# Hybrid decoder trunk: six gate buffers in place of four in the branch merge

## The chip, the cores and the metric

The kernel runs on one core of one Trainium2 chip. The metric is device microseconds (us) of one execution, lower is better. Three runs of the kernel before took 1336.45, 1338.84 and 1338.37 us, so the median is 1338.37 us. A profile was taken of one further execution.

The core has five engines, each with an instruction queue of its own that is worked off strictly in order: TensorE (PE; its weight loads are shown as PEld), VectorE (DVE), ScalarE (ACT), GpSimd (POOL) and SyncE (SP), which here only issues transfers. An instruction that waits holds up all that stand behind it on its engine.

## What is computed

One decoder layer on a 1024 x 1024 input in float32: a norm, one wide projection, two attention branches, a merge of the two by sigmoid gates, an output projection with a residual, and a gated feed-forward part. The change lies in the merge:

```python
y_da = diff_attention(da_q, da_k, da_v, lam, lam_init, subln_w[l])
y_sw = sliding_window_attention(sw_q, sw_k, sw_v, sinks[l])
merged = jax.nn.sigmoid(g_da) * (y_da @ w_br_da[l]) + jax.nn.sigmoid(g_sw) * (y_sw @ w_br_sw[l])
x = x + merged @ w_mix_out[l]
xn = rmsnorm(x, norm_ffn_w[l])
```

`g_da` and `g_sw` are columns of the projection. They were written to HBM before their norm factor was applied (tensor `gd`, 16 rows of 128 x 1024), so the merge loads them, multiplies them by `rstd` and takes the sigmoid.

## The kernel before

Everything is kept transposed: channels on the 128 partitions, the 1024 tokens along the free dimension. A product in full float32 precision is made of three matmuls on high and low parts (`h` and `l` tiles; the high part is a cast on ScalarE, the low part a subtraction on VectorE). 128 output channels are a block, so the merge has 8 blocks, numbered m = 0 to 7 here.

The merge is in `rest`. For each block, `first(m)` takes the next weight (`next_w`, which also has the weight after it loaded and split, lines 177 and 179), allocates two gate tiles of 512 KB with the tag `gr`, loads them on SP (line 796), scales them on GpSimd (line 797), takes the sigmoid on ScalarE (line 804), has TensorE make the 24 matmuls of the first branch (PSUM tile `sc`) and multiplies the first gate by it on VectorE (line 808). `second(m)` makes the 24 matmuls of the second branch in two halves (PSUM tiles `g`, two buffers, lines 212 to 214), multiplies each half of the second gate by it on VectorE (line 816), adds the two gates (line 821; GpSimd for blocks 0 to 5, VectorE for 6 and 7), and splits the sum into the high part `mh` on ScalarE (line 822) and the low part `ml` on VectorE (line 823). `first(0)` and `first(1)` are written ahead of `second(0)`; from block 2 on, `first(m)` and `second(m)` follow each other. TensorE's second-branch product of a block needs the `g` buffer that line 816 of the block before it frees.

The pool of the gate tiles has 4 buffers, two blocks' worth. A buffer is free again when its last reader is done: for a block's second gate that is the add of line 821, for its first gate the subtraction of line 823. The first gate of block m + 2 goes into the buffer of block m's second gate, and the second gate into that of the first.

The order on each engine is not the order of the code: a scheduler that works from estimated times places the instructions of each engine, and the order is then fixed.

After the merge comes `mix`: 8 blocks of 48 matmuls each on `mh` and `ml` (block numbers 0 to 7 again, called mix blocks here). For each, `x2` (a tile of the input, pool `xtp`) is loaded on SP (line 860), the product is added to it on VectorE (line 865), and it is squared, scaled and split for the feed-forward part. `xtp` lies in memory where the merge's pools lay; in the kernel before, the first two `x2` tiles lie just behind the four gate buffers and overlap none of them.

Of the kernel before, what the change touches and what calls it, by code (L numbers as in the profile page):

```python
# [17 lines left out]
P = 128  # L18
D = 1024
T = 1024  # L20
# [24 lines left out]
class Trunk:  # L45
# [723 lines left out]
    def rest(self, gctx):  # L769
        nc, tc = self.nc, self.tc  # L770
        with ExitStack() as ctx:
            e = ctx.enter_context
            mctx = ExitStack()
            mh, ml = [], []
            with gctx, ExitStack() as bctx:
                yrp = bctx.enter_context(tc.tile_pool(name="yrp", bufs=4, reuse_waits="tile"))
                yp = bctx.enter_context(tc.tile_pool(name="yp", bufs=1, reuse_waits="tile"))
                bp = bctx.enter_context(tc.tile_pool(name="bp", bufs=2, reuse_waits="tile"))
                parts = []
                for c in range(8):  # L780
                    with tc.high_priority(200):
                        r = self.tl(yrp, [P, T], "yr")
                        nc.sync.dma_start(r, self.yd[c])
                    parts.append(self.split(*(yp.tile([P, T], F32R, name=f"y{p}{c}") for p in "hl"), r))
                    if self.back[7][0]:
                        self.back_half(*self.back[7][0].pop(0))
                yact = [lambda kc, hf, o=o: [t[:, hf * H2:(hf + 1) * H2] for t in parts[o + kc]] for o in (0, 4)]
                self.xctx.close()
                mp = mctx.enter_context(tc.tile_pool(name="mp", bufs=1, side="right", reuse_waits="tile"))

                def first(m):
                    w = self.next_w()
                    gs = []
                    for br in range(2):
                        g = self.tl(bp, [P, T], "gr", bufs=4)
                        nc.sync.dma_start(g, self.gd[8 * br + m])
                        i = nc.gpsimd.tensor_tensor(g, g, self.rstd, ALU.mult)  # L797
                        if m == 0:

                            tc.add_manual_dep(i.ins, self.last.ins.name, mybir.DependencyInfo(mybir.DependencyClass.Sync, mybir.DependencyReason.DATA),  # L800
                                              reason="softmax first")

                        with tc.issue_after(self.hi.ins) if br else nullcontext():
                            nc.scalar.activation(g, g, AF.Sigmoid)
                        gs.append(g)
                    ps = self.tl(self.psS, [P, T], "sc")
                    self.mm3_both(ps, w, yact[0], range(4), late=() if m else range(4))
                    nc.vector.tensor_tensor(gs[0], gs[0], ps, ALU.mult)
                    return w, gs

                def second(m, w, gs):
                    for hf in range(2):
                        ps = self.tl(self.psG, [P, H2], "g")
                        self.mm3(ps, w, yact[1], hf, range(4), o=4)
                        g = gs[1][:, hf * H2:(hf + 1) * H2]
                        nc.vector.tensor_tensor(g, g, ps, ALU.mult)
                    a = mp.tile([P, T], F32R, name=f"mh{m}")
                    b = mp.tile([P, T], F32R, name=f"ml{m}")
                    with tc.high_priority(30) if m == KC - 1 else nullcontext():
                        for c in [slice(hf * H2, (hf + 1) * H2) for hf in range(2)] if m == KC - 1 else [slice(0, T)]:  # L820
                            (nc.vector if m >= KC - 2 else nc.gpsimd).tensor_tensor(gs[0][:, c], gs[0][:, c], gs[1][:, c], ALU.add)
                            nc.scalar.copy(a[:, c], gs[0][:, c])
                            nc.vector.tensor_tensor(b[:, c], gs[0][:, c], a[:, c].bitcast(F32), ALU.subtract)
                    mh.append(a)
                    ml.append(b)

                both = [first(m) for m in range(2)]
                for m in range(KC):
                    second(m, *(both[m] if m < 2 else first(m)))

            pair = self.mix(mh, ml, mctx)
            self.hidden(pair)
            self.down()
# [626 lines left out]
```

## Time and profile before

| what | value |
|---|---|
| runs | 1336.45, 1338.84, 1338.37 us, median 1338.37 us |
| profiled execution | 1338.85 us, span of its trace 1337.1 us |
| granted TensorE clock | 0.998 |
| busy share of the span | PE 99%, PEld 82%, DVE 79%, ACT 47%, POOL 37% |
| merge, first product to the start of mix | about 506 to 595 us of the span |
| HBM traffic | 130.66 MB read, 50.86 MB written |

In rows of a timeline the columns are the start in us from the start of the span, the length in us, the engine, the line, the operation, output and inputs with their shapes, and the number of instructions that one row merges; in brackets stands how long the engine sat idle before, and what ended that. In the chain of waits the columns are the start, the length and what the chain ran through. A row of waits has the instruction that waited, what it waited for, the total in us, the number of times and the longest one.

### The profile page before, as it was taken

Reading aid. Unit: us, or ns where it says so; the run is one execution under the profiler, and the core shown is the slowest. Engines: PE = TensorE matmul, PEld = TensorE weight load, DVE = VectorE, ACT = ScalarE, POOL = GpSimd, SP = SyncE. Lnnn points to the kernel's source line nnn. Section 1 sums busy time; section 2 is a strip of 40 time slices with the busy share of each in tenths; the row PEclk is TensorE's granted clock in tenths of the full one; section 3 lists DMA queues with packets and bytes.
Section 4 is the critical chain, followed back from the end, with each engine's and each line's share of the span. In section 5 each row is a group of like instructions: output and inputs, shape, how many; then the busy total and the mean of one; then the engine's idle time right before and its main releaser. Section 6 shows DMA issues by size and latency. Waiting matters only on the chain.

```text
span 1337.1 us, 17312 instructions
## 1 busy us (share of the span) xinstructions
PE 1319.5 (99%) x6264; PEld 1096.2 (82%) x6264; DVE 1062.9 (79%) x1601; ACT 623.2 (47%) x1023; POOL 500.9 (37%) x369
## 2 busy tenths in 40 slices
PE   8999999999999999999999999999999999999997
PEld 6888888888888778878888888888888888888887
DVE  8847775289888876456678899999999997878975
ACT  9432232176667765334445443344444444323554
POOL 0336543000002115651436556555565520214532
PEclk9999999999999999999999999999999999999999
DMA  6433443876553335334432222222222229672353
GB/s 259 146 106 145 155 158 142 244 185 177 155 130 121 106 113 210 142 111 144 140 111 82 92 87 87 79 79 95 79 95 71 80 83 327 212 281 73 95 173 126
DMA packets 63622, 183.70 MB, mean 137 GB/s; under 512 B 6960, under 2 KB 15280, under 8 KB 63536
## 3 DMA queue, kind: packets, MB, share of 16 engines
q1 hardware_dynamic: 51504, 164.13, 37.5%
q10 hardware_dynamic: 11456, 17.41, 3.6%
q0 software_dynamic: 576, 1.05, 0.4%
q8 instruction: 49, 0.80, 0.3%
q14 instruction: 37, 0.30, 0.1%
HBM read 130.66 MB, written 50.86 MB: 136 GB/s over the span
## 4 chain that ended last, share of the span: by engine, by line
PE 87%; POOL 4%; DMA 3%; DVE 3%; ACT 1%; issue 1%; POOLq 0%; SPq 0%; ACTq 0%; DVEq 0%
PE t L924 13%; PE t L925 13%; PE t L923 13%; PE t L917 3%; PE sc L639 3%; PE g L212 3%; PE g L213 3%; PE g L214 3%; PE y L1167 2%; PE d L1167 2%; DMA gr<-gd 2%; PE sc L214 2%; PE sc L213 2%; PE sc L212 2%; PE d L924 2%; PE d L923 2%
## 5 line engine op out<-in xcount | busy, mean ns | idle before, releaser
L1097 ACT ACTIVATE c<-us,vecs 128x512 f32<-128x512 f32 x80 | 61.3, 781 | 132.3 <-POOL us L1091 128.3
L1099 DVE SCALAR_TENSOR_TENSOR c<-us,vecs,c 128x512 f32<-128x512 f32 x160 | 110.4, 747 | 8.6 <-ACT c L1097 8.5
L1091 POOL TENSOR_TENSOR us<-us,rstd 128x1024 f32<-128x1024 f32 x38 | 99.6, 2640 | 4.5 <-DVE us L472 2.4
L129 DVE TENSOR_TENSOR sl<-sf,sh 128x1024 fp32r<-128x1024 f32 x62 | 86.6, 1399 | 11.5 <-ACT sh L128 11.5
L128 ACT CAST sh<-sf 128x1024 fp32r<-128x1024 f32 x62 | 63.4, 1047 | 60.3 <-PE t L924 44.0
L179 DVE TENSOR_TENSOR wl<-raw,wh 128x1024 fp32r<-128x1024 f32 (+2 forms) x46 | 56.2, 1221 | 30.7 <-ACT wh L177 19.1
L129 DVE TENSOR_TENSOR wl<-raw,wh 128x1024 fp32r<-128x1024 f32 (+1 forms) x35 | 76.6, 2189 | 3.7 <-ACT wh L128 3.6
L104 POOL TENSOR_TENSOR sf<-rv 128x512 f32<-128x512 f32 x30 | 41.3, 1375 | 101.9 <-DVE sl L129 57.8
L177 ACT CAST wh<-raw 128x1024 fp32r<-128x1024 f32 (+2 forms) x46 | 46.0, 1001 | 59.6 <-PE sc L213 30.5
L212 PE MATMUL g<-xh,wh 128*128 128x512 f32 x176 | 70.7, 401 | 0.1
L214 PE MATMUL g<-xh,wl 128*128 128x512 f32 x176 | 70.4, 400 | 0.0
L213 PE MATMUL g<-xl,wh 128*128 128x512 f32 x176 | 70.3, 400 | 0.0
L109 POOL TENSOR_TENSOR sf<-raw,rv 128x512 f32<-128x512 f32 x30 | 40.7, 1357 | 65.4 <-DVE sl L129 65.4
L622 POOL MEMSET aT<- 128x128 f32 x32 | 6.1, 204 | 151.6 <-PE t L668 97.9
L643 DVE CUSTOM_DVE_ANT_0 L<-sc,bias 128x128 f32<-128x128 f32 (+7 forms) x64 | 47.7, 751 | 17.0 <-PE sc L639 13.8
L644 ACT ACTIVATE L<-L,sm 128x128 f32<-128x128 f32 (+7 forms) x64 | 49.6, 778 | 20.0 <-DVE sm L643 17.3
L797 POOL TENSOR_TENSOR gr<-gr,rstd 128x1024 f32<-128x1024 f32 x16 | 41.0, 2570 | 42.0 <-DMA gr<-gd 41.8
L129 DVE TENSOR_TENSOR wl<-rv,wh 128x512 fp32r<-128x512 f32 x30 | 49.8, 1659 | 3.5 <-ACT wh L128 3.5
L1101 ACT ACTIVATE c<-c 128x512 f32<-128x512 f32 x40 | 24.0, 599 | 60.7 <-DVE c L1099 60.7
L639 PE MATMUL sc<-u,u 128*128 128x512 f32 (+2 forms) x192 | 49.6, 358 | 0.0
L214 PE MATMUL sc<-mh,wl 128*128 128x512 f32 x126 | 49.2, 390 | 0.4 <-DVE wl L179 0.4
L212 PE MATMUL sc<-mh,wh 128*128 128x512 f32 x126 | 49.1, 389 | 0.0
(530 smaller groups left out, 4397.6 us busy)
## 6 DMA issues: line engine op xcount, KB each, us to landing
u<-qd SPq DMA_DIRECT2D x72, 256.0 KB, 6.3
raw<-in_w_in SPq DMA_DIRECT2D x25, 512.0 KB, 4.1
raw<-in_w_up SPq DMA_DIRECT2D x23, 512.0 KB, 3.5
hr<-hd SPq DMA_DIRECT2D x46, 256.0 KB, 5.3
hd<-c SPq DMA_DIRECT2D x22, 512.0 KB, 2.6
rv<-in_w_up SPq DMA_DIRECT2D x21, 512.0 KB, 3.5
raw<-in_w_down SPq DMA_DIRECT2D x19, 512.0 KB, 4.3
gr<-gd SPq DMA_DIRECT2D x16, 512.0 KB, 3.7
```

The lines of the kernel that those rows point to most:

```text
L128: i = nc.scalar.copy(hi, src)
L129: j = nc.vector.tensor_tensor(lo, src, hi.bitcast(F32), ALU.subtract)
L212: nc.tensor.matmul(ps, wh[:, kc + o, :], ah, start=first and n == 0, stop=False)
L213: nc.tensor.matmul(ps, wh[:, kc + o, :], al, start=False, stop=False)
L214: nc.tensor.matmul(ps, wl[:, kc + o, :], ah, start=False, stop=last and n == len(kcs) - 1)
L639: nc.tensor.matmul(sc[:, lo + n0:lo + n1], qs, k[c][part][:, n0:n1], start=part == 0, stop=part == 1)
L923: nc.tensor.matmul(ps, ah[:, k, :], bh, start=first and n == 0, stop=False, skip_group_check=skip)
L924: nc.tensor.matmul(ps, ah[:, k, :], bl, start=False, stop=False, skip_group_check=skip)
L925: i = nc.tensor.matmul(ps, al[:, k, :], bh, start=False, stop=last and n == len(ks) - 1, skip_group_check=skip)
L1091: (nc.vector if j == 0 else nc.gpsimd).tensor_tensor(u[:, 2:], u[:, 2:], self.rstd, ALU.mult)
L1097: nc.scalar.activation(c, u[:, o + 2:o + 2 + H2], AF.Identity, bias=self.vecs[:, C_CB + m:C_CB + m + 1], scale=col(m, 2))
L1099: nc.vector.scalar_tensor_tensor(c, u[:, o + k:o + k + H2], col(m, k), c, ALU.mult, ALU.add)
```

## The change

The gate tiles get 6 buffers in place of 4, 8 KB more in each partition.

```diff
                     gs = []
                     for br in range(2):
-                        g = self.tl(bp, [P, T], "gr", bufs=4)
+                        g = self.tl(bp, [P, T], "gr", bufs=6)
                         nc.sync.dma_start(g, self.gd[8 * br + m])
                         i = nc.gpsimd.tensor_tensor(g, g, self.rstd, ALU.mult)
                         if m == 0:
```

No instruction is added or removed. The first gate of block m + 3 now goes into the buffer of block m's second gate, and the second into that of the first. The two new buffers lie where the first two `x2` tiles of `mix` lie: the first `x2` tile takes the place of the first gate of block 7, the second that of the second gate of block 6, so they can be loaded only when these are done with.

The orders of TensorE and VectorE are the same as before. GpSimd, ScalarE and SP are placed differently. In the rows below the two gates of a block have these numbers: block 0 5078 and 5082, block 1 5118 and 5122, block 2 5224 and 5228, block 3 5297 and 5301, block 4 5370 and 5374, block 5 5443 and 5447, block 6 5516 and 5520, block 7 5589 and 5593.

GpSimd at the beginning of the merge, from the scaling of block 1's gates on, before (L797 scales a gate, L821 adds a block's two gates):

```order
L797 TENSOR_TENSOR gr_5118<-gr_5118,rstd 128x1024
L797 TENSOR_TENSOR gr_5122<-gr_5122,rstd 128x1024
L821 TENSOR_TENSOR gr_5078<-gr_5078,gr_5082 128x1024
L797 TENSOR_TENSOR gr_5224<-gr_5224,rstd 128x1024
L821 TENSOR_TENSOR gr_5118<-gr_5118,gr_5122 128x1024
L797 TENSOR_TENSOR gr_5228<-gr_5228,rstd 128x1024
L797 TENSOR_TENSOR gr_5297<-gr_5297,rstd 128x1024
L797 TENSOR_TENSOR gr_5301<-gr_5301,rstd 128x1024
L821 TENSOR_TENSOR gr_5224<-gr_5224,gr_5228 128x1024
L797 TENSOR_TENSOR gr_5370<-gr_5370,rstd 128x1024
L797 TENSOR_TENSOR gr_5374<-gr_5374,rstd 128x1024
L821 TENSOR_TENSOR gr_5297<-gr_5297,gr_5301 128x1024
```

and the same stretch of the changed kernel:

```order
L797 TENSOR_TENSOR gr_5118<-gr_5118,rstd 128x1024
L797 TENSOR_TENSOR gr_5122<-gr_5122,rstd 128x1024
L797 TENSOR_TENSOR gr_5224<-gr_5224,rstd 128x1024
L797 TENSOR_TENSOR gr_5228<-gr_5228,rstd 128x1024
L821 TENSOR_TENSOR gr_5078<-gr_5078,gr_5082 128x1024
L797 TENSOR_TENSOR gr_5297<-gr_5297,rstd 128x1024
L821 TENSOR_TENSOR gr_5118<-gr_5118,gr_5122 128x1024
L797 TENSOR_TENSOR gr_5301<-gr_5301,rstd 128x1024
L797 TENSOR_TENSOR gr_5370<-gr_5370,rstd 128x1024
L797 TENSOR_TENSOR gr_5374<-gr_5374,rstd 128x1024
L821 TENSOR_TENSOR gr_5224<-gr_5224,gr_5228 128x1024
L797 TENSOR_TENSOR gr_5443<-gr_5443,rstd 128x1024
```

The two scalings of block 2 moved ahead of the add of block 0, and from there on each add stands behind the scalings of the block two after its own; before, it stood behind those of the block one after its own.

ScalarE at the end of the merge, a piece of the difference (L804 is a sigmoid, L177 the cast of a weight: 5510 is the branch weight of block 7, 5583 the first weight of `mix`; L822 makes `mh` of block 5):

```order
+L804 ACTIVATE gr_5589<-gr_5589 128x1024
 L177 CAST wh_5512<-raw_5510 128x1024
 L804 ACTIVATE gr_5520<-gr_5520 128x1024
 L822 CAST mh_5505<-gr_5443 128x1024
-L804 ACTIVATE gr_5589<-gr_5589 128x1024
 L177 CAST wh_5585<-raw_5583 128x1024
 L804 ACTIVATE gr_5593<-gr_5593 128x1024
```

The sigmoid of block 7's first gate moved from just ahead of the cast of the first `mix` weight to just ahead of the cast of the last branch weight.

SP, a piece of the difference around the loads of the first two `x2` tiles (x_992 and x_998):

```order
+L796 DMA gr_5593<-gd 128x1024
+L167 DMA raw_5773<-in_w_mix 128x1024
+L167 DMA raw_5852<-in_w_mix 128x1024
+L167 DMA raw_5919<-in_w_mix 128x1024
 L860 DMA x_992_5710<-in_xT 128x1024
 L860 DMA x_998_5771<-in_xT 128x1024
-L796 DMA gr_5224<-gd 128x1024
-L167 DMA raw_5364<-in_w_br 128x1024
-L796 DMA gr_5228<-gd 128x1024
```

Before, the two `x2` loads stood ahead of the gates of block 2, at the merge's start; now they stand behind the last gate and behind the weights of mix blocks 2 to 4, at the merge's end.

## The prediction

> **What bounds the kernel now.** I read the page first, then TensorE's own idle gaps in the merge, then who waits for whom there, then the chain of waits through it. The page's first part says who sets the end:
>
> ```profile
> PE 1319.5 (99%) x6264; PEld 1096.2 (82%) x6264; DVE 1062.9 (79%) x1601; ACT 623.2 (47%) x1023; POOL 500.9 (37%) x369
> ```
>
> TensorE is busy for 1319.5 of 1337.1 us. A change in the merge can win only what TensorE loses there, and it costs what it makes TensorE lose more. TensorE's timeline between 505 and 700 us has four rows with idle time before them:
>
> ```profile
> 522.89 0.50 PE L212 MATMUL g<-yh,wh 128*128 128x512 f32 x1 [0.44 <-DVE gr L816]
> 577.94 0.50 PE L212 MATMUL g<-yh,wh 128*128 128x512 f32 x1 [0.35 <-DVE gr L816]
> 589.64 0.50 PE L212 MATMUL g<-yh,wh 128*128 128x512 f32 x1 [0.52 <-DVE gr L816]
> 596.24 0.50 PE L214 MATMUL sc<-mh,wl 128*128 128x512 f32 x1 [0.41 <-DVE wl L179]
> ```
>
> That is 1.72 us of idle time; a matmul after a gap is also shown longer than the spacing of 0.23 us, so the loss is up to 0.25 us more for each, some 2.6 us in all. This is the most that can be won: 0.19%. Who waits for whom between 505 and 605 us:
>
> ```profile
> POOL gr L797 <- DMA gr<-gd: 34.1, 10, 11.2
> DVE ml L823 <- ACT mh L822: 24.5, 8, 5.7
> ```
>
> GpSimd waits 34.1 us for gates, and VectorE 24.5 us for the high part of a sum that GpSimd made late. TensorE hardly feels it, but the chain of waits runs through just this loop, not through TensorE:
>
> ```profile
> 523.58 3.26 POOL gr L821
> 526.86 3.20 DMA gr<-gd
> ...
> 533.13 2.41 POOL gr L821
> 535.56 1.06 ACT mh L822
> 536.65 2.34 DVE ml L823
> 539.00 5.04 DMA gr<-gd
> 544.19 2.89 POOL gr L797
> 547.08 2.36 POOL gr L821
> 549.46 3.22 DMA gr<-gd
> ...
> 557.72 3.35 POOL gr L821
> ...
> 563.43 4.50 DMA gr<-gd
> ...
> 570.48 3.35 POOL gr L821
> 573.84 3.28 DMA gr<-gd
> ...
> 582.18 3.34 POOL gr L821
> 585.54 3.69 DMA gr<-gd
> ```
>
> The six L821 rows are the adds of blocks 0 to 5. Each frees a gate buffer, a gate lands there, GpSimd scales it, and only then comes the next add (after the second add the way runs over `mh` and `ml`, which free the other buffer). The adds end at 526.83, 535.54, 549.44, 561.07, 573.83 and 585.52 us: steps of 8.7, 13.9, 11.6, 12.8 and 11.7 us. TensorE's pace is read from the first matmul of block 3's second product and the first of block 4, 24 matmuls later:
>
> ```profile
> 544.79 0.39 PE L212 MATMUL g<-yh,wh 128*128 128x512 f32 x1
> 550.23 0.39 PE L212 MATMUL sc<-yh,wh 128*128 128x512 f32 x1
> ```
>
> That is 5.44 us, 0.2267 each, so a block of 48 takes 10.9 us. So the loop is slower than TensorE, eats TensorE's lead, and from the second product of block 6 on TensorE waits for it. How a late add reaches TensorE is read from VectorE's timeline behind the add of block 5:
>
> ```profile
> 586.63 1.22 DVE L823 TENSOR_TENSOR ml<-gr,mh 128x1024 fp32r<-128x1024 f32 x1 [3.37 <-ACT mh L822]
> 587.77 1.21 DVE L808 TENSOR_TENSOR gr<-gr,sc 128x1024 f32<-128x1024 f32 x1
> 588.90 1.28 DVE L816 TENSOR_TENSOR gr<-gr,g 128x512 f32<-128x512 f32 x2
> ```
>
> The add ends at 585.52, the low part of block 5 follows, and behind it in VectorE's queue stand line 808 and line 816 of block 6, whose first half frees the PSUM buffer. TensorE goes on at 589.64, 4.1 us after the add.
>
> **The change, part by part.** *The loop is not opened.* With six buffers the gates of block m + 3 wait for block m, one block later than before. But on GpSimd each add now stands behind the scalings of the block two after its own, no longer one after. The two shifts cancel: add m frees a buffer, the first gate of block m + 3 lands there, its scaling and that of its sister (which waits for `ml` of block m) come ahead of add m + 1. This is the same cycle, with the same transfers, scalings and casts, as before with m + 2. I therefore take the four steps from the add of block 1 to that of block 5 as unchanged. The step from block 0 to 1 also keeps its form: a landing, one scaling, the add. Nor can the weights' casts come earlier: on ScalarE a branch weight's cast still stands behind a sigmoid whose gate came into the buffer freed by the same add as before.
>
> *The loop starts later.* GpSimd's timeline at the start of the merge:
>
> ```profile
> 517.48 4.78 POOL L797 TENSOR_TENSOR gr<-gr,rstd 128x1024 f32<-128x1024 f32 x2 [11.17 <-DMA gr<-gd]
> 523.58 3.25 POOL L821 TENSOR_TENSOR gr<-gr,gr 128x1024 f32<-128x1024 f32 x1 [1.31 <-DVE gr L816]
> 530.19 2.98 POOL L797 TENSOR_TENSOR gr<-gr,rstd 128x1024 f32<-128x1024 f32 x1 [3.36 <-DMA gr<-gd]
> 535.49 2.41 POOL L797 TENSOR_TENSOR gr<-gr,rstd 128x1024 f32<-128x1024 f32 x1
> ```
>
> The scalings of block 1 end at 517.48 + 4.78 = 522.26, and the add of block 0 begins after 1.31 us of idle time. Now two scalings of block 2 stand between. One lasts 2.41 us undisturbed and 2.98 us beside work of VectorE; VectorE has lines 816 and 179 to do in this stretch, so I take one of each, 5.39 us. The add then begins at 527.65 in place of 523.58: 4.1 us later (3.5 with two short scalings, 4.6 with two long ones). Their gates will be there: they take SP's places of a weight and the two `x2` tiles, which were issued from 511.06 us on, and of those even the slowest landed in 10.2 us:
>
> ```profile
> 511.62 0.98 SPq L860 DMA_DIRECT2D x<-in_xT  x2
> DMA to landing us min/median/max: 3.5/3.9/10.2
> ```
>
> so at 521.8 us. The same rows carry the same 512 KB each, so the gates of block 1 ahead of them land as before. The cost of 4.1 us is carried through five equal steps to the add of block 5, 589.6 us, and from there to TensorE's second product of block 7, 593.7 in place of 589.64. Behind the moved sigmoid of block 2 the cast of that block's weight comes later too. The three instructions of it, before:
>
> ```profile
> 519.93 1.06 ACT L804 ACTIVATE gr<-gr 128x1024 f32<-128x1024 f32 x1 [3.28 <-POOL gr L797]
> 522.26 1.05 ACT L177 CAST wh<-raw 128x1024 fp32r<-128x1024 f32 x1 [1.28 <-PE g L213]
> 523.35 1.22 DVE L179 TENSOR_TENSOR wl<-raw,wh 128x1024 fp32r<-128x1024 f32 x1
> ```
>
> After a scaling that ends near 525 they are done near 528.4, just when TensorE asks for that weight; a wait of some tenths there costs nothing more, since TensorE waits for the loop later anyway.
>
> *The end wins something.* Before, the cast of the first mix weight stood behind the sigmoid of block 7's first gate, which landed only 3.69 us after the add of block 5, and TensorE waited for that weight at 596.24 us. Without a wait this matmul, the third of `mix`, would have come at 589.64 + 24 x 0.2267 + 2 x 0.2267 = 595.5. Now the cast stands behind `mh` of block 5, 1.1 us after the add, and the weight is split some 7 us after the add, while TensorE begins `mix` 4.1 + 5.4 = 9.5 us after it. This wins 0.7 us.
>
> *The `x2` loads.* The first now waits for the last `ml` of block 7. The rows that bear on it:
>
> ```profile
> 604.59 0.69 DVE L823 TENSOR_TENSOR ml<-gr,mh 128x512 fp32r<-128x512 f32 x1
> 607.04 1.22 DVE L865 TENSOR_TENSOR x<-x,sc 128x1024 f32<-128x1024 f32 x1 [1.76 <-PE sc L203]
> 617.92 1.22 DVE L865 TENSOR_TENSOR x<-x,sc 128x1024 f32<-128x1024 f32 x1 [5.57 <-PE sc L214]
> ```
>
> `ml` ended at 605.28; 4 us later gives 609.3. The load lands 3.5 to 5 us behind it, at 613 to 614.5, and line 865 of mix block 0, due near 610.5 now, comes 3 to 4 us late. Behind it in VectorE's queue stands the split of mix block 2's weight, which TensorE wants near 599.1 + 2 x 10.9 = 620.9 us. It would be ready near 617, and the idle 5.57 us before 617.92 cover the rest. On SP, queued behind the waiting load, stand the second `x2` tile and the weight of mix block 5, which TensorE needs over 30 us later. I cost this at nothing; the cover ends when the load lands after about 618.5, and each us beyond costs one.
>
> *The sum.* 4.1 - 0.7 = 3.4 us more. TensorE has no other gap up to 700 us, so nothing behind takes it back. On the profiled execution, 1338.85 us, this makes 1342.25; the median of the runs lies 0.48 us below that execution, so the prediction is 1341.8.
>
> The bounds: two of the loop's steps held late landings, 5.04 and 4.50 us, where others took 3.2 to 3.3. If neither recurs, the loop wins back 1.8 + 1.2 = 3.0 us, and +0.4 is left. If, on the other side, the adds of blocks 1 and 2, which took 2.41 and 2.36 us beside an idle VectorE, take 3.35 like the others, 1.9 us come on top, and with the long scalings 0.5 more: +5.8.
>
> The slow adds have a rule behind them. The Trainium skill's page "SBUF — State Buffer" (the section "Terms") says that VectorE and GpSimd share one pair of ports and that the loser blocks entirely. The trace agrees in part: the `ml` at 536.65 took 2.34 us beside a scaling that ended at 537.90, against 1.22 us elsewhere. By that rule two scalings moved next to VectorE's busy stretch can lose a whole VectorE instruction each, and the sum would be near its upper bound.
>
> **Rivals.** *The gates run ahead, not slower.* If the scalings need not wait for transfers any more, the adds come 8 to 9 us apart, as 535.54 - 526.83 shows for one step, TensorE sets the pace, and all its waits go: at most -2.6, so 1335.8, or 1336 to 1338.5 with part of it. For it speak GpSimd's 34.1 us of waiting; against it that each add is now queued behind scalings of gates which still wait for the add before. It decides only if a step falls below 10.9 us. Chance 0.14. The page "Perfetto Trace Analysis" of the Trainium skill ("Optimization Strategy") holds that the same gap repeating on the engine that should be saturated can mean too few buffers, which is what this change answers; here the repeating gap is on GpSimd, and TensorE's gaps are four. By the rule the sum would be that of this rival.
>
> *Later, but partly taken back.* The late landings do not recur, in part or wholly: +0.3 to +2.2, about 1339.7. For it: they are two of eight or so; against: each comes soon after a weight's load, whose place in SP's queue is unchanged. Chance 0.22.
>
> *VectorE and GpSimd get into each other's way in every step.* Half a us more in each of five steps on top: +4.8 to +8, about 1344.5. For it: four of six adds already last 3.3 us; against: the order on VectorE is the same. Chance 0.14, with the `x2` load's lateness counted in.
>
> **How the numbers follow.** The forecast, +2.2 to +4.8, has 0.50. Its own range is 1340.6 to 1343.2; with the second rival below and the smaller half of the third above, 1338.3 to 1344.3 holds some 0.8. About 0.2%, 2.7 us, can be told from no change, so slower starts at 1341.05: 0.44 of the forecast's 0.50 and the third rival's 0.14 make 0.58. Faster needs the whole of the first rival's gain: 0.06. The rest, 0.36, is within 0.2%.
>
> **What would show it.** Right: the add of block 0 begins near 527.7 us behind four scalings; GpSimd still waits for gates between adds, with steps of 11.5 to 13 us; the add of block 5 ends near 589.6, TensorE's wait before the second product of block 7 ends near 593.7, and there are waits at blocks 4 to 7; the wait for the first mix weight is gone. Wrong: adds less than 11 us apart, an add of block 5 before 587, TensorE without waits at blocks 5 to 7, or a wait at mix blocks 1 to 3 for `x2`.

## The result, and the profile after

| what | before | changed |
|---|---|---|
| median of the runs, us | 1338.34 (1336.45 to 1340.31, 12 runs) | 1341.14 (1340.16 to 1343.11, 12 runs) |
| ratio to before, 95% interval | | 1.0023 [1.0015, 1.003] |
| profiled execution, us | 1338.85 (span 1337.1) | 1340.71 (span 1338.9) |
| granted TensorE clock | 0.998 | 0.998 |

The changed kernel is slower by 2.8 us, with an interval of 2.0 to 4.0 us; 1341.8 was predicted. Two thirds of the loss (1.86 us) stand in the one profiled execution. The first part of its page:

```profile
PE 1320.0 (99%) x6264; PEld 1096.1 (82%) x6264; DVE 1062.4 (79%) x1601; ACT 623.0 (47%) x1023; POOL 501.8 (37%) x369
```

The busy times are those of before within 1 us. No work was added, so the loss must be waiting. TensorE's timeline of the changed kernel, all rows between 505 and 700 us with idle time before them:

```profile
522.76 0.50 PE L212 MATMUL g<-yh,wh 128*128 128x512 f32 x1 [0.41 <-DVE gr L816]
...
556.28 0.50 PE L212 MATMUL g<-yh,wh 128*128 128x512 f32 x1 [0.58 <-DVE gr L816]
...
568.91 0.50 PE L212 MATMUL g<-yh,wh 128*128 128x512 f32 x1 [1.04 <-DVE gr L816]
...
580.59 0.50 PE L212 MATMUL g<-yh,wh 128*128 128x512 f32 x1 [0.50 <-DVE gr L816]
...
592.30 0.50 PE L212 MATMUL g<-yh,wh 128*128 128x512 f32 x1 [0.53 <-DVE gr L816]
```

There are five waits, 3.06 us together, where before had four with 1.72 us. The first, at the second product of block 1, is nearly as before. The others come at the second products of blocks 4 to 7; before, TensorE waited there at blocks 6 and 7 only, and once for the first weight of `mix`. That last wait is gone. With some 0.25 us for each gap that a matmul's length hides (the prediction's estimate), the two lists are 1.6 us apart; the spans are 1.8 us apart.

GpSimd's timeline at the beginning of the merge, changed kernel:

```profile
517.36 9.49 POOL L797 TENSOR_TENSOR gr<-gr,rstd 128x1024 f32<-128x1024 f32 x4 [11.14 <-DMA gr<-gd]
526.80 3.38 POOL L821 TENSOR_TENSOR gr<-gr,gr 128x1024 f32<-128x1024 f32 x1
533.75 2.78 POOL L797 TENSOR_TENSOR gr<-gr,rstd 128x1024 f32<-128x1024 f32 x1 [3.57 <-DMA gr<-gd]
```

Four scalings in a row, 2.37 us each, stand ahead of the add of block 0, which ends at 530.18 in place of 526.83. The chain of waits of the changed kernel from there, with the six adds (L821) and two of the landings between them:

```profile
526.84 3.35 POOL gr L821
...
536.48 2.41 POOL gr L821
...
538.90 4.90 DMA gr<-gd
...
548.81 3.35 POOL gr L821
...
554.52 4.39 DMA gr<-gd
...
561.45 3.34 POOL gr L821
...
573.13 3.35 POOL gr L821
...
584.84 3.34 POOL gr L821
```

The steps from add to add are 8.7, 13.3, 12.6, 11.7 and 11.7 us, in all 58.0 against 58.7 before. The first step is a short one, as before; the other four are still slower than TensorE's 10.9 us for a block, and the loop starts 3.35 us later. Who waits for whom in the changed kernel, 505 to 605 us:

```profile
POOL gr L797 <- DMA gr<-gd: 28.9, 8, 11.1
...
DVE ml L823 <- ACT mh L822: 22.7, 7, 5.7
...
PE g L212 <- DVE gr L816: 3.1, 5, 1.0
```

So GpSimd still waits 28.9 us for gates, although there are two buffers more. Before it was 34.1 us, of which 4.3 us came behind the add of block 5, for the gates of block 7; up to that add the two kernels are about 1 us apart.

### The profile page after: what moved, and what is told of

Its sections match the earlier page's. It is cut to its first block, busy times and chain, and to the rows that moved or that the text cites. A ratio compares the mean times of both kernels' runs of the same rounds, so it can differ in the third digit from the quotient of the medians.

```text
span 1338.9 us, 17301 instructions
## 1 busy us (share of the span) xinstructions
PE 1320.0 (99%) x6264; PEld 1096.1 (82%) x6264; DVE 1062.4 (79%) x1601; ACT 623.0 (47%) x1023; POOL 501.8 (37%) x369
## 4 chain that ended last, share of the span: by engine, by line
PE 87%; POOL 4%; DMA 3%; DVE 3%; issue 1%; ACT 1%; POOLq 0%; SPq 0%; ACTq 0%; DVEq 0%
PE t L925 13%; PE t L923 13%; PE t L924 13%; PE g L212 3%; PE t L917 3%; PE g L213 3%; PE g L214 3%; PE sc L639 3%; PE d L1167 2%; PE y L1167 2%; PE sc L214 2%; PE sc L212 2%; PE d L923 2%; PE d L924 2%; PE sc L213 2%; PE d L925 2%
## 5 line engine op out<-in xcount | busy, mean ns | idle before, releaser
L177 ACT CAST wh<-raw 128x1024 fp32r<-128x1024 f32 (+2 forms) x46 | 46.2, 1003 | 62.3 <-PE sc L213 30.5
L643 DVE CUSTOM_DVE_ANT_0 L<-sc,bias 128x128 f32<-128x128 f32 (+7 forms) x64 | 47.8, 752 | 17.0 <-PE sc L639 13.9
L797 POOL TENSOR_TENSOR gr<-gr,rstd 128x1024 f32<-128x1024 f32 x16 | 39.7, 2495 | 36.7 <-DMA gr<-gd 36.6
L878 POOL TENSOR_TENSOR rstd<-rstd,t 128x512 f32<-128x512 f32 x14 | 21.9, 1572 | 77.7 <-ACT t L877 77.7
```

## The experiments

The theory was this. The two new buffers let the scheduler place each block's scalings one block earlier in GpSimd's fixed queue, ahead of the add that frees the next buffers. The first add is thereby later by two scalings, and every later one still stands behind scalings of gates that wait for the add before it: the loop stays coupled, and nothing takes the delay back. The texts on record name the rivals that each run tells apart: the `x2` loads' new place is what costs (rival A), VectorE and GpSimd block each other more often (rival B), the start is what costs and the loop is not to blame, or there are still too few buffers (rival C).

All medians are of runs beside the kernel before on the same chip. Its median there was 1338.44 us for the scalings behind the add, the late start kept, the delay alone and the late loads, and 1338.55 us for the other four.

**The scalings put behind the add, six buffers.** The same six buffers, but from block 2 on the scaling of block m is issued after the add of block m - 2:

```diff
...
-                        g = self.tl(bp, [P, T], "gr", bufs=4)
+                        g = self.tl(bp, [P, T], "gr", bufs=6)
...
-                        i = nc.gpsimd.tensor_tensor(g, g, self.rstd, ALU.mult)
+                        with tc.issue_after(self.adds[m - 2].ins) if m > 1 else nullcontext(): i = nc.gpsimd.tensor_tensor(g, g, self.rstd, ALU.mult)
...
-                            (nc.vector if m >= KC - 2 else nc.gpsimd).tensor_tensor(gs[0][:, c], gs[0][:, c], gs[1][:, c], ALU.add)
+                            self.adds[m] = (nc.vector if m >= KC - 2 else nc.gpsimd).tensor_tensor(gs[0][:, c], gs[0][:, c], gs[1][:, c], ALU.add)
```

> Six buffers as in the changed kernel, but on GpSimd the scalings of block m are queued behind the add of block m - 2, as in the kernel before. SP's order and the late x2 loads are those of the changed kernel. Theory (the loss is the add of block 0 queued behind two more scalings, kept to the end because each add still stands behind gates that wait for the add before): the add of block 0 ends near 526.8 us again, the next ones find their gates landed, a step costs 3.4 + 2 x 2.4 = 8.2 us, below TensorE's 10.9, so TensorE's waits before the products of blocks 4 to 7 and before the first mix block go and only the one near 522.8 is left: 1336.3 us (1335.5 to 1337.5), faster than both kernels. Rival A (the x2 loads behind the merge and SP's new order cost the time): nothing of that is undone, so 1340.5 to 1342. Rival B (VectorE and GpSimd block each other more often): the same instructions in a tighter sequence, 1339 to 1341.

Measured: 1337.87 us, ratio 0.9993 [0.9984, 1.0001]. GpSimd's timeline of this kernel:

```profile
517.24 4.87 POOL L797 TENSOR_TENSOR gr<-gr,rstd 128x1024 f32<-128x1024 f32 x2 [12.35 <-DMA gr<-gd]
523.43 3.44 POOL L821 TENSOR_TENSOR gr<-gr,gr 128x1024 f32<-128x1024 f32 x1 [1.32 <-ACT wh L177]
526.83 5.76 POOL L797 TENSOR_TENSOR gr<-gr,rstd 128x1024 f32<-128x1024 f32 x2
532.54 3.37 POOL L821 TENSOR_TENSOR gr<-gr,gr 128x1024 f32<-128x1024 f32 x1
```

No scaling waits for a gate any more: after the first pair, no row of GpSimd's until 582 us has idle time that a gate ended. The adds end 9 us apart, until they have caught up with TensorE and follow its 10.9 us. Of TensorE's waits only the first is left, 0.24 us. In this trace the stretch from the start of the first merge product to the start of line 865 of the last mix block takes 174.8 us (506.0 to 680.8) against 177.2 before (506.0 to 683.2). That is 2.4 us less, close to the 2.6 that the prediction set as the most to be won. So the mechanism is as the theory has it, and the change's own six buffers serve once the order is put right; rivals A and B had 1339 us or more here. But the traced execution, 1336.47 us, is the fastest of the eleven. The runs show only a quarter of its gain, 0.6 us, which misses the expected range, and their interval reaches just past 1.0. Against the changed kernel's interval [1.0015, 1.003] it stands clear.

**The same kernel once more**, to see whether that gain repeats:

> The kernel of the run e1_behind once more, for its distance from the kernel before: the trace said 2.4 us less, the runs 0.6. Theory: 2.0 less, 1336.4 us, TensorE without waits from block 2 to the first mix block in this profile too. If what the loop costs the kernel before differs from run to run, or the gain is lost again elsewhere: 0.5 to 1 less, 1337.6.

Measured: 1337.50 us, ratio 0.9991 [0.9982, 1.0]. The theory's 1336.4 was a miss; the second reading, 1337.6, came. GpSimd's timeline and then TensorE's, this execution:

```profile
518.12 5.64 POOL L797 TENSOR_TENSOR gr<-gr,rstd 128x1024 f32<-128x1024 f32 x2 [12.95 <-DMA gr<-gd]
525.09 3.25 POOL L821 TENSOR_TENSOR gr<-gr,gr 128x1024 f32<-128x1024 f32 x1 [1.33 <-DVE gr L816]
```

```profile
524.40 0.50 PE L212 MATMUL g<-yh,wh 128*128 128x512 f32 x1 [1.30 <-DVE gr L816]
```

The loop is open again, without a later wait. But the gate of block 1 landed 0.9 us later, its scalings took 5.64 us, and TensorE's first wait grew from 0.24 to 1.30 us. Here the stretch is 175.9 us, 1.3 us less than before. The gain is 0.6 and 1.1 us in the two sets of runs, smaller than in the trace of each. That wait varies from execution to execution, and the open loop did not take it back here. This would make the runs gain less than the first trace; whether it explains the whole difference stays open.

**The late start kept, the loop opened.** As above, but with the condition from block 3 on (`m > 2` in place of `m > 1`), so that block 2's scalings stay ahead of the add of block 0:

> As the run before, but block 2's two scalings stay ahead of the add of block 0, as in the changed kernel; only from block 3 on are the scalings behind the add of block m - 2. Theory: the add of block 0 ends near 530.2 us, 3.4 late, but with steps of 8.2 us the loop makes this up by block 2 or 3, so TensorE does not wait at blocks 4 to 7: 1336.3 us (1335.5 to 1337.8). So a late start alone would cost nothing; it takes the coupled loop to keep it. A second reading of the same theory (the late start is the loss by itself): 1339.5 to 1341. Rival A: 1340.5 to 1342.

Measured: 1337.58 us, ratio 0.9992 [0.9984, 1.0001]. GpSimd's timeline:

```profile
516.48 9.53 POOL L797 TENSOR_TENSOR gr<-gr,rstd 128x1024 f32<-128x1024 f32 x4 [12.23 <-DMA gr<-gd]
525.97 3.37 POOL L821 TENSOR_TENSOR gr<-gr,gr 128x1024 f32<-128x1024 f32 x1
532.43 3.24 POOL L821 TENSOR_TENSOR gr<-gr,gr 128x1024 f32<-128x1024 f32 x1 [3.09 <-ACT gr L804]
535.63 5.76 POOL L797 TENSOR_TENSOR gr<-gr,rstd 128x1024 f32<-128x1024 f32 x2
```

The same row of four scalings as in the changed kernel, and the add ends at 529.34 us, 2.5 us later than before, although the merge's first product began 0.55 us earlier (505.42); yet TensorE has no wait at all between 500 and 700 us. This trace, too, is of the fastest run (1335.52 us), but the median stands as clear of the change as the one above. A late first add costs nothing if the adds behind it may come at their own pace. The cost needs both parts.

**The start undone, the loop left.** The condition holds for block 2 alone (`m == 2`): the add of block 0 goes back ahead of block 2's scalings.

> Six buffers; only block 2's scalings are put behind the add of block 0, the rest of GpSimd's order is that of the changed kernel, with each add behind scalings two blocks ahead. Theory: the add of block 0 ends near 526.8 again, but three scalings stand between it and the next one, so the add of block 1 comes 1 to 1.9 us later than before; the loop stays coupled, keeps this, and the first mix weight gives 0.7 back: 0.2 to 1.2 more than before, 1338.9 us (1337.8 to 1340). Rival (opening the loop is what helps, wherever it starts): without opening it the changed kernel's loss stays, 1340.5 to 1341.5.

Measured: 1341.06 us, ratio 1.0018 [1.0009, 1.0027], 2.5 us more than before, where the change has 2.8. The expected 1338.9 was a miss; the number is that of the rival beside it, by which the loss stays as long as the loop is not opened. GpSimd's timeline:

```profile
523.62 2.40 POOL L821 TENSOR_TENSOR gr<-gr,gr 128x1024 f32<-128x1024 f32 x1 [1.52 <-ACT wh L177]
525.98 10.09 POOL L797 TENSOR_TENSOR gr<-gr,rstd 128x1024 f32<-128x1024 f32 x3
536.03 2.40 POOL L821 TENSOR_TENSOR gr<-gr,gr 128x1024 f32<-128x1024 f32 x1
```

The add of block 0 ends on time, at 526.02 us. But three scalings follow in one row, 3.36 us each beside VectorE's lines 179 and 823, and the add of block 1 ends at 538.43, 2.9 us later than before. The delay only moved one add on, and the coupled loop carries it to the end as in the change.

**Only the delay, without the buffers.** The kernel before with four buffers, and two multiplications of the scalings' size on a spare tile put ahead of the add of block 0 on GpSimd. Nothing reads their result.

```diff
+    def idle(self, pool, i):
+        d = self.tl(pool, [P, T], "dum", bufs=1)
+        with self.tc.issue_after(i.ins):
+            for _ in range(2):
+                self.idled = self.nc.gpsimd.tensor_tensor(d, self.rstd, self.rstd, ALU.mult)
...
+                            with tc.issue_after(self.idled.ins) if m == 0 else nullcontext(): (nc.vector if m >= KC - 2 else nc.gpsimd).tensor_tensor(gs[0][:, c], gs[0][:, c], gs[1][:, c], ALU.add)
```

> The kernel before, with four buffers, and two more multiplications of 128 x 1024 on GpSimd (rstd by rstd into a spare tile that nothing reads) between the scalings of block 1 and the add of block 0. No gate is loaded earlier, x2 is loaded early as before. Theory: the add of block 0 ends 3.4 us later (two of 2.37 us less 1.3 us of idle time), the loop carries it on, and the wait for the first mix weight stays: 3.4 more, 1341.7 us (1340.3 to 1342.8), TensorE's second product of block 7 near 593. Rival A: nothing that it blames is there, 1338.3. Rival B: two more GpSimd instructions beside VectorE once, at most 1 us, 1338.3 to 1339.4.

Measured: 1341.12 us, ratio 1.0019 [1.001, 1.0027]. GpSimd's timeline, with the added work as L1408:

```profile
517.39 5.68 POOL L797 TENSOR_TENSOR gr<-gr,rstd 128x1024 f32<-128x1024 f32 x2 [12.80 <-DMA gr<-gd]
523.04 4.72 POOL L1408 TENSOR_TENSOR dum<-rstd 128x1024 f32<-128x1024 f32 x2
527.72 2.39 POOL L821 TENSOR_TENSOR gr<-gr,gr 128x1024 f32<-128x1024 f32 x1
```

The add ends at 530.11, as in the changed kernel (530.18), the loop of the kernel before follows it, and the runs lose 2.7 us where the change loses 2.8. In this one execution, 1340.39 us and so 1.5 us above the profile before, the loop gave back about half of the delay: the add of block 5 ends at 587.06, 1.54 us later than before, and TensorE's second product of block 7 begins 1.54 us later (591.18).

In one point this kernel was not as expected. Its `x2` loads were late too; the loads and who waited for them:

```profile
L860 SPq DMA_DIRECT2D x<-in_xT x8: 327/328/425, 606.4 to 670.4; - x8
...
  DVE x L865: 4.4, 1
```

The first of them went out at 606.4 us, where it was 511.6 before; why is not shown, the spare tile may lie in their place. So this run by itself does not part the delay from rival A. The next one does, as it has the late loads without the delay. Taken together, the delay is enough; neither six buffers nor the changed order of the gates' loads is needed for it, and rival B, which had at most 1339.4 us here, falls.

**Only the late `x2` loads.** The kernel before, with the first two `x2` loads made to wait for the last `ml`, as in the change:

```diff
-                            nc.vector.tensor_tensor(b[:, c], gs[0][:, c], a[:, c].bitcast(F32), ALU.subtract)
+                            self.ml = nc.vector.tensor_tensor(b[:, c], gs[0][:, c], a[:, c].bitcast(F32), ALU.subtract)
...
-            nc.sync.dma_start(x2, self.xT[m])
+            j = nc.sync.dma_start(x2, self.xT[m]); i < 2 and tc.add_manual_dep(j.ins, self.ml.ins.name, mybir.DependencyInfo(mybir.DependencyClass.Sync, mybir.DependencyReason.DATA), reason="late")
```

> The kernel before, with four buffers, where the first two x2 loads wait for the last low part of block 7 and stand in SP's queue where the changed kernel has them; GpSimd, ScalarE and VectorE in the order of the kernel before. Theory: costs nothing, TensorE wants the x2 only through the weight queued behind it on VectorE, over 7 us later: 1338.3 us (within 0.7). Rival A: the loss of the changed kernel, 1340.5 to 1341.5.

Measured: 1338.96 us, ratio 1.0001 [0.9992, 1.001]. VectorE's timeline:

```profile
605.68 0.68 DVE L823 TENSOR_TENSOR ml<-gr,mh 128x512 fp32r<-128x512 f32 x1
610.63 1.22 DVE L865 TENSOR_TENSOR x<-x,sc 128x1024 f32<-128x1024 f32 x1 [4.28 <-DMA x<-in_xT]
```

Here line 865 does wait for the load, 4.28 us, and the runs show no difference that is clear of noise (0.5 us, by the interval at most 1.3). The cover that the prediction named (VectorE's idle time before the next mix block) is there, and rival A falls.

**Eight buffers.** `bufs=8` in place of 4, nothing else:

> Eight gate buffers and nothing else changed. On GpSimd three scalings (both of block 2, one of block 3) now stand ahead of the add of block 0, and the adds of blocks 1 to 4 again stand behind scalings of gates that wait for the add before; only the add of block 5 follows that of block 4 directly. Theory: more buffers start the loop still later: three scalings of 2.37 us less 1.3 us of idle time, 5.8 us at the add of block 0, about 6 at the add of block 4, which TensorE feels before the second product of block 6; behind it 1.5 us come back at block 7 and at the first mix weight: 4.5 more than before, 1342.8 us (1341 to 1344.5). Rival C (a deeper pool hides the transfers, and six buffers were too few for it): 1336.5 to 1338.5. Rival A (the x2 loads): as the changed kernel, 1341.

Measured: 1342.05 us, ratio 1.0028 [1.0017, 1.0038]. GpSimd's timeline:

```profile
516.77 13.03 POOL L797 TENSOR_TENSOR gr<-gr,rstd 128x1024 f32<-128x1024 f32 x5 [12.23 <-DMA gr<-gd]
529.77 2.39 POOL L821 TENSOR_TENSOR gr<-gr,gr 128x1024 f32<-128x1024 f32 x1
...
535.56 2.39 POOL L797 TENSOR_TENSOR gr<-gr,rstd 128x1024 f32<-128x1024 f32 x1 [1.03 <-DMA gr<-gd]
```

Five scalings now stand ahead of the first add, which ends at 532.16, 5.3 us later than before, and scalings still wait for gates behind it. More buffers do not help by themselves; rival C falls. The loss of 3.5 us is inside what was expected, and its interval overlaps that of six buffers.

**The gates of block 1 loaded earlier**, to take the first wait away as well. The first kernel of this section, with the loads of block 1's gates given a higher priority:

```diff
-                        nc.sync.dma_start(g, self.gd[8 * br + m])
+                        with tc.high_priority(400) if m == 1 else nullcontext(): nc.sync.dma_start(g, self.gd[8 * br + m])
```

> As e1_behind, and the loads of block 1's gates stand ahead of the last four branch loads (line 783) in SP's queue. The one wait of TensorE left in the merge, 0.2 to 1.7 us near 523 before the second product of block 1, comes from the gate of block 1 that lands at 517 and whose sigmoid VectorE's line 808 needs. Theory: it lands near 504, the wait goes, 0.5 to 1 us less than e1_behind, unless the branch loads, which now go out behind two more transfers, come late for the second product of block 0 at 516.9: 1336.9 us (1335.5 to 1338).

Measured: 1340.53 us, ratio 1.0018 [1.001, 1.0027]: a miss. TensorE's timeline and then VectorE's:

```profile
512.54 0.85 PE L203 MATMUL sc<-yl,wh 128*128 128x512 f32 x2 [1.91 <-DVE yl L837]
513.67 1.22 PE L203 MATMUL sc<-yl,wh 128*128 128x512 f32 x2 [0.29 <-DVE yl L837]
514.69 0.63 PE L212 MATMUL sc<-yh,wh 128*128 128x512 f32 x1
...
516.88 0.39 PE L212 MATMUL sc<-yh,wh 128*128 128x512 f32 x1
```

```profile
502.78 10.84 DVE L837 TENSOR_TENSOR yl<-yr,yh 128x1024 fp32r<-128x1024 f32 x4 [3.57 <-ACT yh L836]
```

Block 1's scalings now run at 505 to 511 us, and there VectorE makes the low parts of the branches (L837). Four of these took 10.84 us. VectorE's timeline of the first kernel of this section, with only two scalings in that place (from 500.12 us, 4.78 us long):

```profile
502.86 6.53 DVE L837 TENSOR_TENSOR yl<-yr,yh 128x1024 fp32r<-128x1024 f32 x4 [3.56 <-ACT yh L836]
```

There four took 6.53 us. With the gates early, TensorE waited 2.2 us for them at the start of the merge. The wait was not the whole loss: behind it the granted TensorE clock was 0.50 from 513.6 to 515.0 us and 0.53 to 516.5, then 1.00 again, and the matmuls came 0.43 us apart in place of 0.23. The second product of block 0 began at 520.98 us, against 516.90 in the first kernel of this section, 4.1 us later. The loop behind was open and without waits, so the time was lost at the merge's start, where there had been no wait. The other cause that the expectation named, the branch loads, ended none of TensorE's waits.

## Why the prediction was right

**The loop is not opened: right.** The steps add up to 58.0 us against 58.7; landings of 4.90 and 4.39 us came again, where before had 5.04 and 4.50. What the prediction took as unchanged gave back 0.7 us, inside the bounds (up to 3.0) that it set. One by one the four steps did change, and the changes partly cancelled: 13.9, 11.6, 12.8 and 11.7 us became 13.3, 12.6, 11.7 and 11.7. The landing of 4.39 now falls into the second of them, where 4.50 fell into the third, and the first no longer runs over `mh` and `ml`, but over the landing, two scalings and an add of 3.35 us in place of 2.36. The runs with the order put right show what an opened loop looks like: 9 us between adds and no wait for gates.

**The loop starts later: right, the size too large.** Predicted was 4.1 us, measured 3.35 at the end of the add. The mis-sized term is one scaling that I took as slowed, 2.98 us; all four took 2.37. The slowed ones stand beside VectorE's lines 179 and 823, and in this stretch VectorE had lines 808 and 816. VectorE's timeline of the changed kernel:

```profile
520.89 1.22 DVE L808 TENSOR_TENSOR gr<-gr,sc 128x1024 f32<-128x1024 f32 x1 [2.49 <-ACT gr L804]
522.03 1.28 DVE L816 TENSOR_TENSOR gr<-gr,g 128x512 f32<-128x512 f32 x2
526.54 1.38 DVE L179 TENSOR_TENSOR wl<-raw,wh 128x1024 fp32r<-128x1024 f32 x1 [3.23 <-ACT wh L177]
...
540.00 2.33 DVE L823 TENSOR_TENSOR ml<-gr,mh 128x1024 fp32r<-128x1024 f32 x1 [5.74 <-ACT mh L822]
```

Lines 808 and 816 read one operand from PSUM; no scaling beside them was slowed. Lines 179 and 823 read two operands from SBUF: the add of block 0 begins beside line 179 and takes 3.38 us, and `ml` at 540.00 takes 2.33 us beside a scaling. The prediction drew on the Trainium skill's page "SBUF — State Buffer" for the loser that blocks entirely, and left out the condition that the page sets in its section "Who interferes with whom": a VectorE instruction with at most one SBUF input, outside the two-port modes, does not contend with GpSimd. These rows agree. The case of two slowed scalings, at the prediction's upper bound, did not arise.

**The end wins something: right.** The wait for the first mix weight is gone. Its split is the row at 594.02 in VectorE's timeline of the changed kernel:

```profile
594.02 1.22 DVE L179 TENSOR_TENSOR wl<-raw,wh 128x1024 fp32r<-128x1024 f32 x1
...
602.66 0.68 DVE L823 TENSOR_TENSOR ml<-gr,mh 128x512 fp32r<-128x512 f32 x1
609.00 1.22 DVE L865 TENSOR_TENSOR x<-x,sc 128x1024 f32<-128x1024 f32 x1 [5.65 <-PE sc L203]
```

The split ends at 595.24, 7.1 us after the add of block 5 (588.17), as worked out. TensorE's second product of block 7 came 2.66 us later than before (592.30 against 589.64), line 865 of mix block 0 only 1.96 us later (609.00 against 607.04): 0.7 us won between them.

**The `x2` loads cost nothing: right, but not for the reason given.** Line 865 was predicted to wait 3 to 4 us for its load, behind VectorE's cover. It waited for TensorE, and not for the load. The last `ml` ended at 603.34 us and not at 609.3: I moved it with the add of block 5, while in the changed kernel block 7's gates were scaled before that add (579.96 us) and no longer after it, so the work between the add and the last `ml` became 4.6 us shorter (15.2 against 19.8 us). The cover, which the change did not need, is shown by the run with late loads alone.

**The sum.** By this one execution: 3.35 later at the first add, 0.7 back in the loop, 0.7 at the end, 1.95 in all; the spans are 1.8 us apart, the profiled times 1.86. The medians are 2.8 us apart. TensorE's wait at block 7 ended at 592.30, where 593.7 was predicted. The difference of the 1.95 to the predicted 3.4 is 0.75 at the first add and 0.7 in the loop. So the mechanism is shown by the traces, while the nearness of the median to the forecast is in part luck: the two traced executions, taken alone, lie below the forecast's +2.2 to +4.8. The one before was 0.5 us above the median of its runs and the changed one 0.4 below, which makes up the 0.9 us between the two figures; the executions of either kernel scatter by 3 to 4 us.

**The rivals.** The gates running ahead, the first rival, did not happen, but its mechanism exists: with the add placed first on GpSimd, the same six buffers give it. It was worth 0.6 and 1.1 us in the runs, with intervals that reach 1.0, where 2.6 was set as the most (its terms add up to 2.7). "Later, but partly taken back" has the number of the one trace, but not its reason, as the late landings did recur; the runs' median lies in the forecast's range. VectorE and GpSimd did not get more into each other's way in every step: of the adds that had been short, that of block 2 took 3.39 us, and that of block 1 2.40 as before.

## What to carry to other kernels

A deeper buffer pool also changes the order in the fixed queues: prefetch work that was held back by a buffer is placed earlier, and can land ahead of the one instruction that frees the next buffers. Before adding buffers, look at what each in-order engine will run ahead of that instruction, and put the prefetched work behind it. Here the loop that was slower than the bottleneck carried much of a late start to its end (2.66 of 3.35 us in the changed kernel's trace, 1.54 of 3.28 in that of the delay alone), and the loop that was faster forgot it; so of two edits, the one that shortens the loop's step comes first.

## What the runs showed of the hardware that was not expected

One and the same GpSimd instruction, 128x1024 in float32 with two inputs in SBUF, took 2.37 to 2.42 us alone or beside VectorE work that reads PSUM, and up to 3.4 us beside VectorE work that reads two operands from SBUF. In the pair that can be compared best, the one that began second lost the time. In the kernel before, the split of a weight on VectorE (line 179) began at 523.35 us and took its 1.22 us, and the add of block 0, which began at 523.58, took 3.25. With the start undone the add began first, at 523.62, and took 2.40, and the split took 3.46; VectorE's timeline there:

```profile
523.64 3.46 DVE L179 TENSOR_TENSOR wl<-raw,wh 128x1024 fp32r<-128x1024 f32 x1 [0.17 <-ACT wh L177]
```

In the kernel with the gates loaded earlier this turned a prefetch into a TensorE wait of 2.2 us, and some 3 us of matmuls at a granted clock of 0.50 to 0.53 followed. Behind the single waits of up to 1.8 us in the other kernels (1.72 with the late `x2` loads, 1.76 with eight buffers) the granted clock stayed at 1.00.

In executions of kernels whose work before the merge is the same (all but the one with the gates loaded earlier), the merge's first product began between 505.4 and 506.6 us, the scalings of block 1's gates between 516.5 and 518.6 us, and TensorE's first wait in the merge was between nothing and 1.7 us. In the coupled loop TensorE waits for the loop later anyway; in the open loop this first wait is what remains.
